# One weight load for consecutive matmuls on the same weight tile, in a streaming encoder on eight cores

## The chip, the cores and the metric

The kernel runs on all 8 NeuronCores of one Trainium2 chip. Two dies hold four cores each (cores 0 to 3 and 4 to 7). Each core works through a share of the tokens of its own, with the whole set of weights; the cores exchange nothing. The metric is the device time of the slowest core, in microseconds (us).

This program has two states. In the fast state all eight cores are granted nearly the full TensorE clock and the time is near 14830 us. In the slow state the cores of one die, or of both, are granted less (a mean of 0.829 on one die in a run of 17575.37 us, 0.97 in one of 15204.02 us), and the time is up to 20% longer. Times below are compared fast run with fast run, or on the cores of a die that was not slowed, and the text says which.

## The reference

Two layers of an encoder, at model width 2048, on 2 x 16384 new tokens and 16 x 16 continued ones. What matters here is the list of matrix products of one layer:

```python
h = rmsnorm(x, norm_mix_g)
z = h @ w_in                      # 2048 -> 12288: branch inputs and four gates
# ... four branches: convolutions, spatial gating, pooling; each ends in a 512 -> 2048 product
merged = gate0 * a_out + gate1 * b_out + gate2 * c_out + gate3 * d_out
x = x + merged @ w_o              # 2048 -> 2048
h2 = rmsnorm(x, norm_ffn_g)
x = x + (silu(h2 @ ffn_w1) * (h2 @ ffn_w3)) @ ffn_w2      # 2048 -> 5632 -> 2048
```

## The kernel before

Each core takes its tokens in five blocks of 768 to 896 columns per layer, with the channels on the 128 partitions. A matmul holds a weight tile in the array (the stationary operand; 128 x 128 in 83562 of the 83602 that the profile counts) and streams columns past it, 512 at most in this program. A block is cut into two halves `s = 0, 1` of 384, 400 or 448 columns, and both halves follow each other on the same weight tile. Everything that TensorE does goes through one helper:

```python
def mm(bank, lo, hi, lhsT, rhs, start, stop, rc, M=128):
    pe(lambda e, o=psum[0:M, bank, lo:hi], a=lhsT, b=rhs: e.matmul(o, lhsT=a, rhs=b, start=start, stop=stop),
       rc, [("p", bank)])
    est["pe"] += max((hi - lo) / 2400.0 + 0.003, 0.139)
```

`pe` records the instruction with what it reads and writes; the waits are derived from that. `e.matmul` issues two instructions, a weight load and a matmul (the profile counts 83602 of each). The main callers are these:

```python
def mm_cols(p, ws, wo_, nk, rhs_of, subs=(0, 1), ks=None, nks=None):     # most products
    ks = range(nk) if ks is None else ks
    nks = nk if nks is None else nks
    for k in ks:
        for s in subs:                       # both halves on weight tile k
            r, rc, nn = rhs_of(k, s)
            mm(2 * p + s, 0, nn, ws.ap[:, k, wo_:wo_ + 128], r, k == 0, k == nks - 1, ...)

def mm_tiles(tiles, nk, rhs_of):             # a few passes that take one half at a time
    for k in range(nk):
        for (bank, s, ws, wo_) in tiles:     # another weight tile each time
            ...

def w2_mm(banks, og, kg, sub, first, last):  # the last product
    # ... [cut]
    for mi in range(4):
        for j in range(KG):
            for s in sub:                    # sub = (0, 1) in nearly all calls
                ...
```

## Time and profile before

| | before |
|---|---|
| fast runs of the first three | 14828.32 and 14831.11 us (the other one was slow: 17679.49) |
| span of the slowest core in the profile | 14827.8 us |
| TensorE matmuls: number, busy | 83602, 14696.9 us (99%) |
| weight loads: number, busy | 83602, 8172.2 us (55%) |
| VectorE, ScalarE busy | 32%, 15% |

These are lines of the profile page of the kernel before, on its slowest core, as all views here where no core is named. First the span, then busy time by engine with its share and the number of instructions (PE is the matmuls, PEld the weight loads, which overlap them: 14696.9 and 8172.2 us in a span of 14827.8). Then the granted clock in 40 slices of the span, in tenths, where 9 is 90% or more. Then the chain of work that ended last, as shares of the span by line (the view breaks this long line off). Last come the two costliest groups: count, busy us, mean ns of one, idle time of the engine before them and what ended most of it.

```profile
span 14827.8 us, 199596 instructions; the slowest of 8 cores (14795.9 to 14827.8 us)
...
PE 14696.9 (99%) x83602; PEld 8172.2 (55%) x83602; DVE 4759.0 (32%) x5309; ACT 2150.6 (15%) x2983; POOL 187.1 (1%) x382
...
PEclk9999999999999999999999999999999999999999
...
PE psum L426 97%; DMA arena<-wsA 1%; DMA arena<-xin 0%; DMA arena<-std 0%; DMA arena<-wpA 0%; DVE arena L898 0%; DVE arena L644 0%; DVE arena L609 0%; DVE arena L979 0%; ACT L636 0%; DMA arena<-maskS 0%; DMA arena<-stb 0%; DVE arena L1262 0
...
L426 PE MATMUL psum<-arena 128*128 128x448 bf16 (+3 forms) x83602 | 14696.9, 339 | 115.3 <-ACT arena L620 38.4
L426 PEld LDWEIGHTS psum<-arena 128*128 128x128 bf16 x83602 | 8172.2, 98 | 6639.5 <-issue 161.9
```

The reader is to see that matmuls fill the span and that the chain consists of them, at full clock. The question is whether the other large number, 8172 us of loads, is inside the matmul time or beside it. Groups by shape (columns as above) let one compute the pace, because matmul records overlap and their union is the busy time:

```profile
L426 PE MATMUL psum<-arena 128*128 128x448 bf16 x32904 | 6237.6, 353 | 10.3 <-DVE arena L1231 6.1 <-DMA arena<-wsA 3.7 <-ACT arena L636 0.2
L426 PE MATMUL psum<-arena 128*128 128x400 bf16 x24644 | 4182.6, 333 | 23.2 <-DMA arena<-wsA 12.6 <-ACT arena L620 4.2 <-DVE arena L1231 4.0
L426 PE MATMUL psum<-arena 128*128 128x384 bf16 x24020 | 3912.8, 326 | 10.7 <-DMA arena<-wsA 6.4 <-DVE arena L1231 3.7 <-ACT arena L636 0.7
```

For the three main shapes busy time over count is 6237.6 / 32904 = 189.6 ns, 169.7 ns and 162.9 ns. The distances from the start of one matmul to the start of the next, taken from the trace's records, have medians of 189, 169 and 162 ns, and 56 ns between the 128-column matmuls, which come in short groups. All lie on columns / 2.4 + 2.5 ns, a line put through these medians: the 320 columns from 128 to 448 add 133 ns, 0.416 ns each. The mean of 326 to 353 ns in the lines is the length of one record, whose end is modelled by the profiler; it is not the pace.

The timeline at 5000 us (start us, length us, engine, what) merges equal instructions; six matmuls and five loads fill the same stretch:

```profile
4999.80 1.14 PE L426 MATMUL psum<-arena 128*128 128x384 bf16 x6
4999.97 0.75 PEld L426 LDWEIGHTS psum<-arena 128*128 128x128 bf16 x5
```

Five loads start within 0.75 us, that is one in every 162 ns, each 0.10 us long and 2 ns after the start of a matmul. Lastly the waits of TensorE in the whole run (us in total, times, longest us), the two longest:

```profile
PE psum L426 <- ACT arena L620: 38.4, 3, 22.1
PE psum L426 <- DMA arena<-wsA: 22.7, 5, 10.0
```

They are short; no line of this view speaks of weights that were late in the array (the DMA line is a transfer into on-chip memory). The view knows only waits for semaphores, so the paces above are the stronger evidence.

### The profile page before, as it was taken

How to read it: one execution, taken by the hardware profiler on the slowest of the kernel's cores; microseconds unless marked ns; L12 is line 12 of the kernel's file. 1: busy time of each engine (PE TensorE's matmuls, PEld its weight loads, DVE VectorE, ACT ScalarE, POOL GpSimd, SP SyncE). 2: the span in 40 equal slices, each digit the busy share in tenths (PEclk: the TensorE clock that was granted, in tenths of full speed). 3: DMA queues.
4: the chain of work that ended last, by engine and by line, in shares of the span. 5: the costliest groups of instructions: out<-in, count | busy, mean ns of one | idle time of the engine just before them, and what ended most of it. 6: DMA issues, size and time to landing. Idle time of an engine off the chain costs nothing.

```text
span 14827.8 us, 199596 instructions; the slowest of 8 cores (14795.9 to 14827.8 us)
## 1 busy us (share of the span) xinstructions
PE 14696.9 (99%) x83602; PEld 8172.2 (55%) x83602; DVE 4759.0 (32%) x5309; ACT 2150.6 (15%) x2983; POOL 187.1 (1%) x382
## 2 busy tenths in 40 slices
PE   8999999999999999999999999999999999999999
PEld 4555555555555656555556655555555555665555
DVE  7211621162214321522162125311632153216311
ACT  2110211011101110111021002100211011102100
POOL 0000000000000000000000000000000000000000
PEclk9999999999999999999999999999999999999999
DMA  9898565443545454545533252424243334343423
GB/s 202 192 199 202 121 146 139 148 148 119 146 133 165 137 166 163 151 144 156 168 128 123 107 178 102 158 86 149 110 156 111 115 140 169 126 156 124 161 107 119
DMA packets 326745, 2138.75 MB, mean 144 GB/s; under 512 B 55648, under 2 KB 64416, under 8 KB 229600
## 3 DMA queue, kind: packets, MB, share of 16 engines
q1 hardware_dynamic: 303552, 1821.87, 34.6%
q0 software_dynamic: 22304, 304.11, 12.4%
q8 instruction: 670, 10.98, 0.3%
q14 instruction: 219, 1.79, 0.0%
HBM read 2160.76 MB, written 436.92 MB: 175 GB/s over the span
## 4 chain that ended last, share of the span: by engine, by line
PE 97%; DMA 1%; DVE 1%; issue 0%; ACT 0%; SPq 0%; DVEq 0%; ACTq 0%; POOLq 0%
PE psum L426 97%; DMA arena<-wsA 1%; DMA arena<-xin 0%; DMA arena<-std 0%; DMA arena<-wpA 0%; DVE arena L898 0%; DVE arena L644 0%; DVE arena L609 0%; DVE arena L979 0%; ACT L636 0%; DMA arena<-maskS 0%; DMA arena<-stb 0%; DVE arena L1262 0%; SPq L393 0%; ACT arena L1158 0%
## 5 line engine op out<-in xcount | busy, mean ns | idle before, releaser
L426 PE MATMUL psum<-arena 128*128 128x448 bf16 (+3 forms) x83602 | 14696.9, 339 | 115.3 <-ACT arena L620 38.4
L426 PEld LDWEIGHTS psum<-arena 128*128 128x128 bf16 x83602 | 8172.2, 98 | 6639.5 <-issue 161.9
L1325 DVE TENSOR_TENSOR arena<-psum,arena 128x896 bf16<-128x896 f32 (+2 forms) x400 | 408.7, 1022 | 4079.9 <-PE psum L426 4079.9
L1231 DVE TENSOR_TENSOR arena<-psum,arena 128x896 f32<-128x896 f32 (+2 forms) x640 | 636.7, 1016 | 2328.4 <-PE psum L426 2326.6
L898 DVE SCALAR_TENSOR_TENSOR arena<-arena 128x896 f32<-128x896 f32 (+4 forms) x1200 | 1242.1, 1095 | 49.1 <-ACT arena L895 33.1
L1213 ACT ACTIVATE arena<-psum 128x896 bf16<-128x896 f32 (+2 forms) x640 | 550.9, 861 | 3458.3 <-PE psum L426 3399.4
L1317 ACT ACTIVATE arena<-psum 128x896 f32<-128x896 f32 (+2 forms) x400 | 344.4, 861 | 4012.6 <-PE psum L426 4012.6
L644 DVE SCALAR_TENSOR_TENSOR arena<-arena 128x448 bf16<-128x448 f32 (+10 forms) x592 | 442.9, 800 | 570.2 <-DMA arena<-xs 330.8
L609 DVE TENSOR_TENSOR arena<-arena 128x896 f32<-128x896 f32 (+7 forms) x414 | 339.2, 819 | 791.8 <-ACT arena L608 774.5
L608 ACT ACTIVATE arena<-arena 128x896 f32<-128x896 f32 (+7 forms) x414 | 302.7, 732 | 1224.0 <-DVE arena L1262 368.9
L1236 DVE TENSOR_TENSOR arena<-arena 128x896 f32<-128x896 f32 (+5 forms) x480 | 466.5, 1013 | 0.0
L1380 DVE TENSOR_TENSOR arena<-psum,arena 128x896 f32<-128x896 f32 (+2 forms) x156 | 159.5, 1022 | 792.7 <-PE psum L426 792.7
L729 DVE TENSOR_TENSOR arena<-arena 128x768 f32<-128x768 f32 (+1 forms) x60 | 61.5, 1025 | 306.2 <-ACT arena L728 306.2
L497 POOL DMA_DIRECT2D wsA<-wpA x216 | 104.4, 487 | 4029.3 <-PE psum L426 4002.7
L1260 DVE TENSOR_TENSOR arena<-psum,arena 128x896 f32<-128x896 f32 (+2 forms) x80 | 81.5, 1019 | 212.2 <-PE psum L426 212.2
L606 ACT ACTIVATE arena<-arena 128x896 f32<-128x896 f32 (+4 forms) x22 | 19.1, 866 | 763.7 <-DMA arena<-xs 251.5
L640 DVE RECIPROCAL arena<-arena 128x448 f32<-128x448 f32 (+4 forms) x38 | 103.3, 2746 | 78.0 <-ACT arena L636 78.0
L1262 DVE TENSOR_TENSOR arena<-psum,arena 128x448 f32<-128x448 f32 (+2 forms) x160 | 93.3, 583 | 64.7 <-PE psum L426 64.7
L979 DVE TENSOR_TENSOR arena<-arena 128x910 f32<-128x910 f32 (+13 forms) x100 | 104.0, 1040 | 6.2
L1121 DVE SCALAR_TENSOR_TENSOR arena<-arena 128x896 f32<-128x896 f32 (+4 forms) x80 | 87.1, 1089 | 55.9 <-ACT arena L1118 51.4
L863 ACT COPY arena<-arena 128x30 f32<-128x30 f32 (+2 forms) x96 | 14.7, 201 | 587.3 <-PE psum L426 587.2
L1328 DVE TENSOR_TENSOR arena<-psum,arena 128x448 bf16<-128x448 f32 (+2 forms) x80 | 46.7, 583 | 165.3 <-PE psum L426 165.2
(84 smaller groups left out, 1614.6 us busy)
## 6 DMA issues: line engine op xcount, KB each, us to landing
arena<-wsA SPq DMA_DIRECT2D x450, 2048.0 KB, 8.9
arena<-wsW SPq DMA_DIRECT2D x145, 1408.0 KB, 6.4
wsA<-wpA POOLq DMA_DIRECT2D x216, 512.0 KB, 11.2
arena<-wpA POOLq DMA_DIRECT2D x50, 2048.0 KB, 21.4
wsA<-arena SPq DMA_DIRECT2D x46, 2048.0 KB, 20.1
arena<-wsO SPq DMA_DIRECT2D x144, 512.0 KB, 6.1
arena<-xs SPq DMA_DIRECT2D x160, 448.0 KB, 6.4
arena<-xs SPq DMA_DIRECT2D x128, 384.0 KB, 5.5
```

The costliest lines, as they stand in the source:

```text
L426: pe(lambda e, o=psum[0:M, bank, lo:hi], a=lhsT, b=rhs: e.matmul(o, lhsT=a, rhs=b, start=start, stop=stop), rc, [("p", bank)])
L497: s=wsrc[k][l, i, j * r:(j + 1) * r].rearrange("p (q m) -> p q m", q=4): e.dma_start(out=o, in_=s),
L608: act(lambda e: e.activation(out=sq.ap[:, 0:hi - lo], in_=x_ap, func=AF.Square), xc, sq.cells(None, 0, hi - lo))
L609: eng_add(lambda e: e.tensor_tensor(out=acc.ap[:, lo:hi], in0=acc.ap[:, lo:hi], in1=sq.ap[:, 0:hi - lo], op=ALU.add), acc.cells(None, lo, ...
L644: dve(lambda e: e.scalar_tensor_tensor(out=out_ap, in0=x_ap, scalar=gcol, in1=rs.ap[:, lo:hi], op0=ALU.mult, op1=ALU.mult), xc + rs.cells( ...
L898: dve(lambda e: e.scalar_tensor_tensor(out=ac.ap[:, 0:CWa], in0=ex.ap[:, k:k + CWa], scalar=w, in1=ac.ap[:, 0:CWa], op0=ALU.mult, op1=ALU. ...
L1213: act(lambda e, p=p, mi=mi, q=sgq: e.activation(out=two(q[mi].ap), in_=pap(p, hf), func=AF.Sigmoid), [], sgq[mi].cells(), pk(p))
L1231: dve(lambda e, p=p, mi=mi, dst=dst, q=sgq: e.tensor_tensor(out=two(dst.ap), in0=pap(p, hf), in1=two(q[mi].ap), op=ALU.mult), sgq[mi].cell ...
L1236: dve(lambda e, mj=mj, dst=dst: e.tensor_tensor(out=dst.ap, in0=macc[mj].ap, in1=mtmp[mj % 2].ap, op=ALU.add), macc[mj].cells() + mtmp[mj ...
L1317: act(lambda e: e.activation(out=two(t.ap), in_=pap(p, hf), func=AF.Silu), [], t.cells(), pk(p))
L1325: dve(lambda e: e.tensor_tensor(out=two(hid[f].ap), in0=pap(p, hf), in1=two(t.ap), op=ALU.mult), t.cells(), hid[f].cells(), pk(p))
L1380: dve(lambda e: e.tensor_tensor(out=two(x.ap), in0=pap(p, hf), in1=two(x.ap), op=ALU.add), x.cells(), x.cells(), pk(p))
```

## The change

The intent is to leave out the load where the array already holds the tile: the second half of each pair reuses the weights of the first. Python keeps the key of the tile last loaded; a partial tile (fewer than 128 rows or columns) clears it.

```diff
+    held = [None]
+
     def mm(bank, lo, hi, lhsT, rhs, start, stop, rc, M=128):
-        pe(lambda e, o=psum[0:M, bank, lo:hi], a=lhsT, b=rhs: e.matmul(o, lhsT=a, rhs=b, start=start, stop=stop),
-           rc, [("p", bank)])
+
+        key = (lhsT.offset, tuple(map(tuple, lhsT.ap)))
+        if held[0] == key:
+            pe(lambda e, o=psum[0:M, bank, lo:hi], a=lhsT, b=rhs: e.add_instruction(mybir.InstMatmult(
+                name=nc.get_next_instruction_name(), engine=mybir.EngineType.PE, ins=[e.lower_ap(b), e.lower_ap(a)], outs=[e.lower_ap(o)],
+                start_tensor_calc=start, stop_tensor_calc=stop, tile_size=(128, 128), tile_position=(0, 0), ldweights=False)),
+               rc, [("p", bank)])
+        else:
+            pe(lambda e, o=psum[0:M, bank, lo:hi], a=lhsT, b=rhs: e.matmul(o, lhsT=a, rhs=b, start=start, stop=stop),
+               rc, [("p", bank)])
+        held[0] = key if M == 128 and rhs.shape[0] == 128 else None
         est["pe"] += max((hi - lo) / 2400.0 + 0.003, 0.139)
```

## The prediction

> **What bounds the kernel now.** TensorE, by its moving columns. In the page of the slowest core (span 14827.8 us) matmuls are busy 14696.9 us (99%), and the chain that ended last is 97% "PE psum L426"; VectorE is busy 32%, ScalarE 15%. The granted clock is 0.997 or 0.998 on all cores. Idle time before matmuls is only 115.3 us.
>
> Weight loads look large (83602, 8172.2 us busy, 55%), but they overlap. I took the start-to-start distance of consecutive matmuls from the trace's records of core 2. Median: 128 columns 56 ns, 384 columns 162, 400 columns 169, 448 columns 189, 512 columns 216. Every one of these matmuls has a load of its own. One line fits all: columns / 2.4 per ns + 2.5 ns. A load is recorded at 98 ns and starts about 2 ns after the start of the matmul before the one that needs it; next to 162 to 189 ns it is over long before. The few 128-column matmuls even run at 56 ns with a load each. No matmul waits for its weights.[...]
>
> **What the change does.** The built program keeps its matmuls (83602, same order and shapes); 38349 no longer load: the second of 38159 pairs, plus the runs of 4 and 16 on the constant averaging weights. Loads fall to 45253, recorded load time to about 45253 x 98 ns = 4430 us (30%). Not paired: the passes that go through tiles one half at a time, and the 512-column ones whose stationary side is the activations. Nothing moves on VectorE, ScalarE, the DMA queues or in the semaphores.
>
> **How much of that is critical.** The removed 3.75 ms of load time lie under matmuls: zero. What could be critical is the 2.5 ns per matmul beyond the columns. If all of it were the exchange of weights, 38349 x 2.5 ns = 96 us (0.65%) would go. [...] in this trace every matmul loads, so it can't tell the two apart. I give the exchange about 15%. The load of the next pair now stands behind two matmuls; even if it can only start with the second, 98 ns fit in 162.
>
> **Prediction.** 14822 us (fast state), range 14740 to 14850. Faster by over 2%: 0.01; within 2%: 0.96; slower by over 2%: 0.03.
>
> **What would show it.** Right: load instructions 45253 and load busy about 30%; matmul count and busy time as before; start-to-start of 384/400/448 columns still 162/169/189 ns, for the second of a pair as for the first; the chain still 97% PE. Shifted: the second of a pair at 160/167/187 ns, then about 96 us less. Wrong: a start-to-start over 200 ns within pairs, or new idle time before matmuls.
>
> **What would make it wrong.** A matmul without a load may cost something that no record here shows: if the load of the next pair can't start before the second matmul has ended, each pair would pay up to one load, 38159 x (56 to 98 ns) = 2.1 to 3.7 ms. I think this unlikely, as loads are seen running under matmuls already. [...] the slower state (17679 us, one run of three) may come more or less often; that is no part of this number.

## The result

Results are correct, with 38349 matmuls that use a tile held from the one before. Before and after ran six times each:

| | before | after |
|---|---|---|
| fast runs | 14823.86, 14828.32, 14831.11 us | 14827.33, 14832.66 us, and one more of 14861.95 us outside the six |
| slow runs | 16796.42, 17234.72, 17679.49 us | 15282.33, 16327.08, 16631.47, 16735.94 us, and one more of 16600.72 us outside the six |
| median of all six | 15813.76 us | 15804.7 us |
| ratio of fast runs, 95% interval | | 1.0009, 0.9986 to 1.0031 |

Ratios in this document are the mean time of one kernel's fast runs over the mean of the other's fast runs of the same rounds, so they are not quite the ratio of the medians that are quoted. Here 14840.6 / 14827.8 = 1.0009. The time in the fast state did not change. The medians, which mix the two states, lie a thousand microseconds above either kernel's fast time.

The lines of the profile page after the change that answer to those of before (same columns; L436 is now the matmul with a load, L431 the one without):

```profile
span 14831.0 us, 161247 instructions; the slowest of 8 cores (14794.4 to 14831.0 us)
...
PE 14697.0 (99%) x83602; PEld 4422.7 (30%) x45253; DVE 4759.7 (32%) x5309; ACT 2154.9 (15%) x2983; POOL 187.1 (1%) x382
...
PE psum L436 52%; PE psum L431 45%; DMA arena<-wsA 1%; DMA arena<-std 0%; DMA arena<-xin 0%; DVE arena L655 0%; DVE arena L909 0%; DVE arena L620 0%; DVE arena L990 0%; SPq L393 0%; ACT L647 0%; DMA arena<-maskS 0%; DMA od<-arena 0%; ACT ar
...
L436 PE MATMUL psum<-arena 128*128 128x448 bf16 (+6 forms) x45253 | 14186.9, 339 | 102.8 <-ACT arena L631 47.1
L431 PE MATMUL psum<-arena 128*128 128x448 bf16 (+3 forms) x38349 | 12961.0, 339 | 15.7 <-ACT arena L1169 13.4
L436 PEld LDWEIGHTS psum<-arena 128*128 128x128 bf16 (+1 forms) x45253 | 4422.7, 98 | 10391.8 <-issue 9818.6
```

38349 loads are gone (161247 instructions in place of 199596), recorded load time fell from 8172.2 to 4422.7 us, and matmul busy time is 14697.0 against 14696.9 us. The chain is 97% TensorE as before, now split over two lines (52% and 45%). The busy times of the two matmul lines can't be added or divided into a pace, as each overlaps the other. The timeline of the same stretch gives it:

```profile
4999.75 0.33 PE L436 MATMUL psum<-arena 128*128 128x384 bf16 x1
4999.92 0.33 PE L431 MATMUL psum<-arena 128*128 128x384 bf16 x1
4999.92 0.10 PEld L436 LDWEIGHTS psum<-arena 128*128 128x128 bf16 x1 [0.23 <-issue]
5000.08 0.33 PE L436 MATMUL psum<-arena 128*128 128x384 bf16 x1
5000.24 0.33 PE L431 MATMUL psum<-arena 128*128 128x384 bf16 x1
5000.24 0.10 PEld L436 LDWEIGHTS psum<-arena 128*128 128x128 bf16 x1 [0.23 <-issue]
```

Matmuls with and without a load alternate, and both start 0.16 us after the one before. A load now starts together with the *second* matmul of a pair (4999.92, 5000.24): the next tile's load stands behind that matmul in the program and starts when it starts (2 ns later in the median of the records). From the records of the whole core, the median start-to-start by columns and kind:

| columns | before, each with a load | after, from the loading one to its partner | after, from the partner to the next loading one |
|---|---|---|---|
| 384 | 162 ns | 163 ns | 162 ns |
| 400 | 169 ns | 169 ns | 169 ns |
| 448 | 189 ns | 189 ns | 189 ns |

(The means of the undisturbed ones at 384 columns are 162.50, 162.52 and 162.48 ns; records are in whole ns.)

### The profile page after: what moved, and what is told of

The parts are those of the page before. It is cut to its first block, busy times and chain, and to the rows that moved or that the text cites. A ratio compares the mean times of both kernels' runs of the same rounds, so it can differ in the third digit from the quotient of the medians.

```text
span 14831.0 us, 161247 instructions; the slowest of 8 cores (14794.4 to 14831.0 us)
## 1 busy us (share of the span) xinstructions
PE 14697.0 (99%) x83602; PEld 4422.7 (30%) x45253; DVE 4759.7 (32%) x5309; ACT 2154.9 (15%) x2983; POOL 187.1 (1%) x382
## 4 chain that ended last, share of the span: by engine, by line
PE 97%; DMA 1%; DVE 1%; issue 0%; ACT 0%; SPq 0%; DVEq 0%; ACTq 0%
PE psum L436 52%; PE psum L431 45%; DMA arena<-wsA 1%; DMA arena<-std 0%; DMA arena<-xin 0%; DVE arena L655 0%; DVE arena L909 0%; DVE arena L620 0%; DVE arena L990 0%; SPq L393 0%; ACT L647 0%; DMA arena<-maskS 0%; DMA od<-arena 0%; ACT arena L1169 0%; ACT arena L647 0%
## 5 line engine op out<-in xcount | busy, mean ns | idle before, releaser
L436 PE MATMUL psum<-arena 128*128 128x448 bf16 (+6 forms) x45253 | 14186.9, 339 | 102.8 <-ACT arena L631 47.1
L431 PE MATMUL psum<-arena 128*128 128x448 bf16 (+3 forms) x38349 | 12961.0, 339 | 15.7 <-ACT arena L1169 13.4
L436 PEld LDWEIGHTS psum<-arena 128*128 128x128 bf16 (+1 forms) x45253 | 4422.7, 98 | 10391.8 <-issue 9818.6
L508 POOL DMA_DIRECT2D wsA<-wpA x216 | 104.5, 487 | 4037.8 <-PE psum L431 3627.8
```

The costliest lines, as they stand in the source:

```text
L431: pe(lambda e, o=psum[0:M, bank, lo:hi], a=lhsT, b=rhs: e.add_instruction(mybir.InstMatmult(name=nc.get_next_instruction_name(), engine=my ...
```

## The experiments

The theory H: each removed load ran under a matmul, and the 2.5 ns beyond the columns belong to the matmul. Rivals: X, the exchange of weights costs the 2.5 ns; R, there was a saving, given back because loads now start later; S, a load takes its recorded 98 ns of the load path, so the path was more than half full and the kernel near its limit. All of the first four ran on one chip and share the runs of before: 11 counted, three fast, 14829.68, 14830.81 and 14834.6 us.

### The change once more

No edit.

> The changed kernel once more, unaltered, against before in the same rounds. Theory H (every removed load lay under a matmul, and the 2.5 ns beyond the columns belong to the matmul, not to the exchange of weights): fast runs at 14825 to 14832 us, ratio 1.000 +- 0.002. Rival X (a skipped exchange saves the 2.5 ns): 96 us less, ratio 0.9935. Slow runs will be among them for both kernels and are not compared.

Fast runs: 14828.25 and 14830.74 us; ratio 0.9999, interval 0.9969 to 1.0028 (recorded as "unclear"; it rests on two fast runs against three). Theory H holds; X's 0.9935 lies outside. Six of its eight runs were slow, and so were eight of the eleven of before. The profile of this run fell in the slow state. The view of the cores shows what that is (us, mean granted clock):

```profile
core 0: 15089.1 us, clock 0.978
...
core 4: 16713.1 us, clock 0.874
```

The four cores of one die were at 0.874 and took 16713 to 16739 us, those of the other at 0.978 to 0.979 and took 15058 to 15089 us: the time goes with the clock. This profile is used for nothing else.

### A load at the first matmul of a group alone

Results are wrong: all products of an accumulation use the first weight tile.

```diff
-        if held[0] == key:
+        if held[0] == key or (held[0] is not None and not start and M == 128 and rhs.shape[0] == 128):
```

> A load only at the first matmul of each accumulation group, none after (wrong results on purpose): about 3386 loads in place of 83602, 4%. Theory H: loads are worth nothing even when nearly all are gone: fast runs at 14820 to 14835 us, start-to-start still 162/169/189 ns. Rival X (exchange costs 2.5 ns): 80200 x 2.5 ns = 200 us less, 14630 us. Rival R (the saving of the pairs was given back because the load of the next pair now starts only with the second matmul): removing nearly all loads would then take the rest away, well under 14800 us.

3386 loads are left. The only fast run took 14835.62 us. The profile fell in a slow run, but only die 0 was slowed; these are lines of the page of core 6, on the other die (clock 0.997):

```profile
span 14825.4 us, 119353 instructions; the slowest of 8 cores (14797.3 to 16182.0 us)
...
PE 14694.4 (99%) x83575; PEld 322.3 (2%) x3386; DVE 4757.4 (32%) x5309; ACT 2150.9 (15%) x2983; POOL 187.1 (1%) x382
```

The loads are down to 322.3 us (2% of the span), the span of that core is 14825.4 us, and the medians of the start-to-start on it are still 162, 169 and 189 ns. So even all loads together were worth nothing: X (200 us) and R fall. Being a single fast run it carries no interval, but the paces are those of some 80000 matmuls.

### Two loads for each matmul

```diff
+        if M == 128 and rhs.shape[0] == 128:
+            pe(lambda e, a=lhsT: e.ldweights(a), rc, [])
         pe(lambda e, o=psum[0:M, bank, lo:hi], a=lhsT, b=rhs: e.matmul(o, lhsT=a, rhs=b, start=start, stop=stop),
            rc, [("p", bank)])
```

> The kernel before with one more load of the same tile ahead of each matmul's own: 167164 loads. Theory H with loads pipelined (they can follow each other in 56 ns or less, as the 128-column matmuls showed): two loads take at most 112 ns, under the 162 ns of the shortest main matmul: 14825 to 14835 us. Rival S (a load occupies the array's load path for its recorded 98 ns, one after the other): two take 196 ns, start-to-start 196 ns for 384, 400 and 448 columns, that is 24020 x 34 + 24644 x 27 + 32904 x 7 ns = about 1.7 ms more, 16.5 ms.

Correct, fast runs 14830.23 and 14832.06 us, ratio 1.000 (0.9971 to 1.0029; again two fast runs against three, recorded as "unclear"). Lines of its page (L427 is the extra load):

```profile
span 14828.6 us, 283158 instructions; the slowest of 8 cores (14796.0 to 14828.6 us)
...
PE 14702.7 (99%) x83602; PEld 11456.6 (77%) x167164; DVE 4759.3 (32%) x5309; ACT 2151.9 (15%) x2983; POOL 187.5 (1%) x382
...
L427 PEld LDWEIGHTS <-arena 128*128 128x128 bf16 x83562 | 8173.3, 98 | 3330.8 <-issue 114.3
L428 PEld LDWEIGHTS psum<-arena 128*128 128x128 bf16 x83602 | 7977.5, 96 | 25.3 <-issue 21.9
```

Loads are now busy 77% of the span, and the time is that of 55%, of 30% and of 2%. Rival S would have cost 1.7 ms: it falls. Two loads go with nearly every matmul, and matmul busy time over count is 14702.7 / 83602 = 175.9 ns, under the 196 ns of two records. A load's 98 ns is the length of its record, not the time for which it keeps the next load out.

### Doses of loads

This measures the slack: 1, 3, 5 and 9 extra loads ahead of each gate matmul, by quarter of that stage, in the second layer, each dose on a line of its own.

```diff
+        for _ in range(dose[0]):
+            pe(lambda e, a=lhsT: e.ldweights(a), rc, [])
 ...
+                    dose[0] = (1, 3, 5, 9)[mg] if l == 1 else 0
                     mm_cols(p, ws, mi * 128, KC, rF)
+                    dose[0] = 0
```

> In the gate stage of the second layer, 1, 3, 5 and 9 extra loads of the same tile ahead of each matmul (its own still follows), by quarter of the stage; nothing else changed. Read from the start-to-start of the matmuls of 384, 400 and 448 columns. Theory H, with a load's repeat time t of at most 56 ns: dose 1 stays at 162/169/189 ns; from the dose where (1+extra) x t passes that, the start-to-start is (1+extra) x t: with t = 56 ns it is 224, 336 and 560 ns at 3, 5 and 9 extra; with t = 27 ns (an estimate from the few 32-column matmuls, 25 ns apart with a load each) only 9 extra passes it, at 270 ns. Rival S (98 ns each, in series): 196, 392, 588 and 980 ns.

The profile is a fast run. Groups by shape, for 384 columns only, costliest first: L431 is one extra load, L433 three, L435 five, L437 nine.

```profile
L437 PE MATMUL psum<-arena 128*128 128x384 bf16 x1024 | 345.1, 337 | 40.6
...
L435 PE MATMUL psum<-arena 128*128 128x384 bf16 x1024 | 223.9, 339 | 3.6 <-DVE arena L1245 3.6
...
L431 PE MATMUL psum<-arena 128*128 128x384 bf16 x1024 | 168.0, 326 | 0.0
L433 PE MATMUL psum<-arena 128*128 128x384 bf16 x1024 | 167.7, 326 | 0.0
```

One and three extra loads cost nothing: 168.0 / 1024 and 167.7 / 1024 are 164 ns, and the medians are 162 ns. The medians at five and nine extra are 217 and 377 ns, and these are the same for 384, 400 and 448 columns: there loads set the pace. Ten loads against six are 160 ns more, so a load repeats every 40 ns. Both fit n x 40 - 23 ns for n loads in all; two numbers in it were taken from two measurements, so the fit is no test of it, but the records show the 40 ns directly: inside a run of nine, most loads start 39 or 40 ns after the one before. The timeline within the last dose shows it:

```profile
13000.02 0.42 PEld L429 LDWEIGHTS <-arena 128*128 128x128 bf16 x9
13000.38 0.10 PEld L437 LDWEIGHTS psum<-arena 128*128 128x128 bf16 x1
13000.40 0.42 PEld L429 LDWEIGHTS <-arena 128*128 128x128 bf16 x9
```

The first of nine loads in a run starts at 13000.02 and the first of the next nine at 13000.40. The expectation was off on the size: neither 56 nor 27 ns (an estimate; the few 32-column matmuls of before start 25 to 28 ns apart), but 40 ns. By this law four loads take 137 ns and hide (162 ns was measured at 384 columns with three extra), five would take 177 ns (an estimate from the fit); the kernel before used one. The whole agrees as well: 2560 matmuls at 217 and 2560 at 377 ns in place of 162, 169 and 189 come to 626 us, and the one fast run took 15457.78 us (the other run was slow, 18138.59 us), 626 us over the mean of the three fast runs of before.

### Narrow matmuls: where a held tile could pay

In one block of the second layer the 384-column matmuls of the channel mixer are cut into pieces of 128, 64 or 32 columns, in another form for each weight group, each form on lines of its own (results stay correct). Elsewhere this kernel holds tiles as after the change.

```diff
+        def mm_split(p, ws, wo_, rhs_of, width, every, M, extra, form):
+            for k in range(KC):
+                i = 0
+                for s in (0, 1):
+                    r, rc, nn = rhs_of(k, s)
+                    for c in range(0, nn, width):
+                        # [cut: extra loads, then form(...), with a load where i % every == 0]
+                        i += 1
```

> In one block of the second layer the gated matmuls of 384 columns are cut into pieces, another form for each weight group, read from the start-to-start: 128, 64 and 32 columns with a load each, the same with one load per weight tile (6, 12, 24 pieces), 64 columns with one load for two, 64 and 32 columns with two loads each. The doses gave a start-to-start of n x 40 - 23 ns where n loads per matmul bind (217 at 6, 377 at 10). Law B takes that down to n = 1: 17 ns, so a load each never binds: 56, 29 and 25 ns (the 25 seen for 32 columns in the kernel before), the same held or not; with two loads 57 ns for 64 and for 32 columns. Theory C: a load needs its 40 ns each: 56, 40 and 40 ns with a load each, 56, about 30 and 26 held, so there the change would pay by up to a third; two loads 80 ns or 57 ns.

All three runs were slow, so only the die that was not slowed in one of them is read, and its medians. Its clock of 0.989 to 0.990 is below that of fast runs because of stretches at half clock in the forms below (the longest on core 7 has 220.4 us at 0.50). Groups by shape on core 7: at 64 columns L460 has a load each and L470 holds; at 32 columns L484 and L494; L500 and L508 have two loads each.

```profile
L508 PE MATMUL psum<-arena 128*128 128x32 bf16 x3072 | 224.4, 207 | 0.0
...
L500 PE MATMUL psum<-arena 128*128 128x64 bf16 x1536 | 88.9, 203 | 0.0
L484 PE MATMUL psum<-arena 128*128 128x32 bf16 x3072 | 81.2, 178 | 13.9 <-issue 13.5
L494 PE MATMUL psum<-arena 128*128 128x32 bf16 x2944 | 76.9, 176 | 0.0
...
L460 PE MATMUL psum<-arena 128*128 128x64 bf16 x1536 | 48.2, 196 | 5.4 <-issue 5.4
...
L470 PE MATMUL psum<-arena 128*128 128x64 bf16 x1408 | 44.9, 193 | 0.0
```

Medians of the start-to-start are 56, 29 and 25 ns at 128, 64 and 32 columns, with a load each as well as held, and 29 ns with one load for two pieces of 64. With two loads each at 64 columns it is 58 ns, where the law gives 57. So Law B (the same law for one load) stands against C: a single full load hides even under 32 columns, as far as the pace goes. A tenth form, 384 columns whole with a load each, ran last, at 163 ns.

Two things did not fit at first sight. With two loads at 32 columns the median is 73 ns and not 57. The records divide that stretch in two. The first 65 distances, at full clock, are 57 to 59 ns, as the law says; after 3.8 us the granted clock fell to 0.5, and from there they are 73 ns. The stretches before and after the fall (us of the stretch, busy us of PE, PEld, DVE, ACT and POOL with the instructions in brackets, granted clock, DMA share and GB/s):

```profile
13217.70:13221.40 3.70, 3.70 (x68) 3.70 (x132) 0.96 (x1) 0.00 (x0) 0.00 (x0) 1.00 0.69 208
13221.50:13441.90 220.40, 220.40 (x3009) 220.40 (x6014) 2.87 (x3) 3.25 (x4) 0.00 (x0) 0.50 0.07 25
```

And at 64 and 32 columns the forms with a load each do lose time that the held ones don't: 5.4 and 13.9 us of idle time, nearly all put down to "issue", and a granted clock of 0.94 and 0.93 over their stretches against 1.00. In all they took 53.4 us against 44.7 held, and 94.8 against 76.6. The other three cores of the die show it too (4.2 to 4.8 and 13.2 to 15.2 us). The lost clock goes with the gaps: on core 7 at 32 columns it fell to 0.5 for 3.4 us four times, each within 1.6 us of the end of a gap of 1.3 to 3.2 us. The gaps of over 0.2 us lie 127 or 128 matmuls apart, or two or three times that, on all four cores, and the held forms have none. What makes the gaps was not tested.

### Narrow matmuls with weight tiles of 96 columns

The same block with 96 columns of weights in the tile, held or not (wrong results).

> The same block with weight tiles of 96 columns in place of 128 (wrong results on purpose)[...]: 384, 128, 64 and 32 moving columns, with a load each and with one load per weight tile. If such a load repeats no slower than the full one: 162, 56, 29 and 25 ns, held or not, as in the run with 128. If it repeats at about the time recorded for a load (98 ns): 162 and 162 at 384 columns (still hidden, no gain from holding), but 98 ns with a load each at 128, 64 and 32 columns against 56 to 65, 30 to 40 and 25 to 30 ns held: there, and only there, holding the weights pays.

A fast run (clock 0.989 to 0.990, with the stretch at half clock that is shown below; the only run of before in this series was slow). Groups by shape: at 384 columns L444 loads each time and L454 is the partner that doesn't; at 64 columns L476 loads each time and L486 holds; at 32 columns L492 and L502.

```profile
L492 PE MATMUL psum<-arena 128*96 128x32 bf16 x3072 | 243.2, 240 | 0.0
...
L502 PE MATMUL psum<-arena 128*96 128x32 bf16 x2944 | 79.8, 176 | 0.0
...
L476 PE MATMUL psum<-arena 128*96 128x64 bf16 x1536 | 69.3, 209 | 0.0
L486 PE MATMUL psum<-arena 128*96 128x64 bf16 x1408 | 46.9, 193 | 0.0
...
L444 PE MATMUL psum<-arena 128*96 128x384 bf16 x256 | 41.8, 326 | 0.0
...
L454 PE MATMUL psum<-arena 128*96 128x384 bf16 x128 | 41.6, 326 | 0.0
```

With 384 and with 128 columns nothing changes: 162 and 56 ns, loaded or held. With 64 columns the start-to-start is 45 ns with a load each, and held it is 45 ns once after a load and 29 ns for the rest. That is 69.3 us against 46.9 us for the same work: here a held tile pays a third. The figure expected for such a load was wrong (98 ns; it is 45 where it binds), and so was the other case that was named, a repeat no slower than the full tile's. Its record is longer too: 125 ns at 64 columns, against 100 ns for the full tile in the run before. For 32 columns the next view has the same columns as the last one, for the stretches at 64 columns loaded, 32 loaded (in two parts) and 32 held:

```profile
12911.30:12980.30 69.00, 69.00 (x1537) 69.00 (x1534) 3.83 (x4) 3.24 (x4) 0.00 (x0) 1.00 0.18 64
13027.30:13030.80 3.50, 3.50 (x84) 3.50 (x80) 0.96 (x1) 0.00 (x0) 0.00 (x0) 1.00 0.70 197
13030.90:13270.20 239.30, 239.30 (x2995) 239.30 (x2993) 2.87 (x3) 3.24 (x4) 0.00 (x0) 0.50 0.04 16
13270.30:13349.80 79.50, 79.50 (x3068) 15.50 (x129) 3.83 (x4) 3.24 (x4) 0.00 (x0) 0.98 0.15 55
```

At 32 columns the median is 80 ns loaded and 25 held, but only the second part of the loaded stretch is at half clock. The first 78 distances, at full clock, are 45 ns; after 3.5 us the clock fell to 0.5 and they became 80 ns. So the load alone makes 45 ns out of 25, and the clock makes 80 out of 45. What lowered the clock was not tested. It fell in the two forms that streamed 32 columns only every 45 or 57 ns, and stayed at 1.00 where 64 columns came every 45 or 58 ns and at 32 held columns every 25 ns (with full tiles). As an estimate from the line through the medians of the kernel before, columns / 2.4 ns, the columns fill 30% and 23% of the time in the first two, and 59%, 46% and 53% in the others.

### Control: fewer columns, all loads kept

```diff
-                    mm_cols(p, w1s, fi * 128, KC, r2)
+                    mm_cols(p, w1s, fi * 128, KC, r2, cut=32)      # [cut: the same for w3s and w2]
```

> Control on the other term of the sum: the kernel before, all loads kept, but 39680 of the matmuls of the channel mixer stream 32 columns fewer (wrong results on purpose). If the columns set the pace, each is 32 / 2.4 = 13.3 ns shorter: 39680 x 13.3 ns = 529 us less, fast runs at 14300 us, ratio 0.964. If the loads (98 ns each, 83602 of them) or the instruction rate had any share in the pace, the gain would be smaller or absent.

> The changed kernel in the same rounds as the control with fewer columns: fast runs within 0.3% of before (14820 to 14840 us), while the control gains 3.6%.

With fewer columns (wrong results) the fast runs took 14300.64 and 14308.11 us (two others were slow), ratio 0.9626 (0.9589 to 0.9663). Lines of its page:

```profile
span 14299.0 us, 199596 instructions; the slowest of 8 cores (14266.7 to 14299.0 us)
...
PE 14168.8 (99%) x83602; PEld 8172.7 (57%) x83602; DVE 4759.5 (33%) x5309; ACT 2150.3 (15%) x2983; POOL 187.1 (1%) x382
```

Its 83602 loads are busy 8172.7 us as before, and matmul busy time fell by 14696.9 - 14168.8 = 528 us, against 529 expected. The change in the same rounds took 14852.65 and 14859.68 us in its fast runs, before 14828.01 to 14894.49 us in five; this chip spread more. The two are 13 and 20 us above the upper end that was expected, and inside before's spread; their mean over before's is 14856.2 / 14855.5 = 1.000, worked out from these runs, as no interval was formed for this pair. Columns are worth time, loads are not.

## Why the prediction was right or wrong

- **What bounds the kernel: right.** Matmul columns set the pace. The control took 32 columns out of 39680 matmuls and gained 528 us of matmul busy time, 13.3 ns each.
- **What the change removes: right.** 45253 loads are left, 4422.7 us (4430 said), nothing else moved.
- **None of it is critical: right.** The means of the fast runs agree within 0.1%, and the pace is 162/169/189 ns with and without a load.
- **The 2.5 ns: open in the prediction, now settled for the exchange.** It was given 15%, the author's estimate, that they were the exchange of weights. A matmul that exchanges nothing has the same pace (162.52 ns from its predecessor at 384 columns, against 162.50 before), so they are not.
- **The stated danger did not come.** It was feared that the next load could wait for the end of the second matmul. It starts with that matmul's start (2 ns after it), and 98 ns of record, or 40 ns of repeat time, fit under its 162 ns.
- **The number: wrong, by the step that left out the slow state.** The prediction said "14822 us (fast state), range 14740 to 14850", and that the slower state "is no part of this number". The measured figure is the median of six runs, 15804.7 us, and four of those were slow. The step that failed is to give a range for the fast state alone after one slow run in three had been seen; the term left out was the share of slow runs. It is worth 975 us in this median (15804.7 less 14830.0, the mean of the two fast runs of the six). It is no mark of the change: the kernel before, with three slow of six, has 15813.76 us. Against the fast runs, the number was off by some 8 us. The range held the two of the six; 14861.95 us, and 14852.65 and 14859.68 us on the chip that spread more, lie above it.
- **Left open.** Why a run becomes slow. Counted over the runs behind the medians, 14 of 25 of before were slow (3 of 6, 8 of 11, 1 of 1, 2 of 7), 13 of 19 of the change (4 of 6, 6 of 8, 3 of 5), 5 of 7 with doubled loads, 7 of 8 with almost none. The slow state was there whether a program had 167164 loads or 3386, and these counts are too few to say if its share differs.

## What to carry to other kernels

Judge a weight load by how often loads can follow each other, against the columns of the matmul above it, and not by its recorded length or its busy share: here full 128-column loads repeat in 40 ns and one of them hid under any matmul tried (start-to-start of 56, 29 and 25 ns at 128, 64 and 32 columns, loaded or held), so that leaving out nearly half of them, nearly all, or doubling them gave the same time (fast runs of 14824 to 14862 us in the first two series). Keeping a tile can pay where matmuls are narrow: with 96-column tiles and 64 moving columns it took a third off (46.9 against 69.3 us), and with full tiles at 64 and 32 columns it avoided some stalls (44.7 against 53.4 us and 76.6 against 94.8 us; each seen in one run). When a kernel has two clock states, predict both the time in each and the share of the slow one, since a median of few runs follows the share (here 15804.7 us with four slow of six, 14830.0 us as the mean of the two fast ones).
